# A decoder step on one core: the first stage with half-size first pieces, more warm-up matmuls, small vectors on the GpSimd queue and a pinned order

## Chip, cores and metric

One core of a Trainium2 chip runs the whole step. The metric is device time in microseconds of one execution; the median of several runs is compared. TensorE does the matrix products and transposes, VectorE (DVE), ScalarE (ACT) and GpSimd (POOL) the rest; SyncE (SP), ACT and POOL issue the DMAs.

## What is computed

One layer of a hybrid decoder for 256 prompt tokens and 8 x 8 sample tokens (320 columns in all). The input is normalised, one combined projection feeds two branches (mLSTM and gated linear attention), both are merged by gates, and a gated ConvFFN follows:

```python
h = _rmsnorm(x, norm_mix_w)
proj = h @ _f32(w_in)
mq, mk, mv, mo, mi, mf, gq, gk, gv, gr, gal, gate_a, gate_b = jnp.split(proj, split_at, axis=-1)
...
merged = (jax.nn.sigmoid(gate_a) * (y_m @ _f32(w_branch_a))
          + jax.nn.sigmoid(gate_b) * (y_g @ _f32(w_branch_b)))
x = x + merged @ _f32(w_out)
```

Only the first stage is touched in the source: the load and transposition of x, the token scale `rsqrt(mean(x*x) + EPS)`, and the first two products gq and gk with 256 columns of `w_in` each.

## The kernel before, in words

Every product is done in three passes: a weight block `raw` (128 x 4 x 256, 512 KB) is split by ACT into a rounded part `wh` (line 69) and by DVE into the rest `wl` (line 70); x is kept likewise as `hH[k]` and `hL[k]`, one tile of 128 x 320 for each of 16 row blocks k. TensorE adds `wh*hH`, `wh*hL` and `wl*hH` (lines 74, 75, 76). `raw` has 4 buffers, `wh` and `wl` 3 each, and PSUM has 4 `big` banks (products) and 4 `mx` banks (all else).

The start: 8 warm-up matmuls of ones (line 110), then x is loaded in four column pieces (`x_load`, lines 144 and 145, SP queue), each piece transposed by TensorE in 4 tiles k (`x_chunk`, line 153: two matmuls for the prompt, one for the sample tokens, each recorded as two), from which ACT writes `hH[k]` (154), DVE `hL[k]` (155), and both a plain copy `xT` (158, 160). Weight pieces `first(C_GQ, c)` and `first(C_GK, c)` alternate with the x pieces on SP. A piece c gives 48 products: 4 k x 2 halves x 3 passes for gq, and the same for gk; the stage has 192 products and 16 transposed tiles.

`token_scale` (called for c == 3, lines 163 to 176): ACT squares x with a running sum (168), DVE scales (169), POOL takes the power (170), DVE spreads the result over `lh` (174), TensorE transposes it (175), DVE copies it to `rstd_bc` (176). gq and gk are evacuated with `rstd_bc` (129). Then ten small vectors come in on the SP queue (204 to 213) and are transposed into `vecT` and `cwT` (215 to 217). Behind the stage a gate block `graw` is loaded on the ACT queue and split with POOL's memsets (319, 320) and ACT's small casts (322).

Later, at some 90 to 115 us, the rows `we` (391, 392) are written to DRAM by POOL (403, 404), read back as `bc` (647), and used by DVE in `qi` (658); the same DVE queue frees the PSUM banks of TensorE's level matmuls (568) with predicated copies (571).

What sets the order: the program is recorded in the order of the code, and a scheduler with its own timeline then orders each engine's queue; every engine runs its queue in that order. Eight DMA semaphores for hardware queues go round, so that a ninth issue waits until the transfer eight before it has landed.

Of the kernel before, what the change touches and what calls it, by code (L numbers as in the profile page):

```python
# [24 lines left out]
N = T + NS  # L25
# [7 lines left out]
RAW = 4  # L33
NWARM = 8
# [9 lines left out]
def step_kernel(ctx: ExitStack, tc: tile.TileContext, a: dict):  # L44
# [9 lines left out]
    def mx(name="mx"):  # L54
        return ps.tile([P, 512], F32, tag="mx", name=name)
# [4 lines left out]
    w_in = a["w_in"][0]  # L60

# [40 lines left out]
    nc.vector.memset(onec, 1.0)  # L102
    mhalf = cp.tile([P, 3], F32, name="mhalf")
# [3 lines left out]
    nc.scalar.activation(warm, onec, AF.Copy)  # L107
# [24 lines left out]
    with tc.tile_pool(name="st", bufs=1) as st:  # L132
        vrow = st.tile([P, 3, P], F32, name="vrow")
        nmr = st.tile([16, P], F32, name="nmr")
        nc.scalar.dma_start(nmr, a["norm_mix_w"].rearrange("o (k p) -> (o k) p", p=P))
        nmw = st.tile([P, 16], F32, name="nmw")
        pv = mx("mx1")
        nc.tensor.transpose(pv[:, :16], nmr, ident[0:16, 0:16])
        nc.vector.tensor_copy(nmw, pv[:, :16])
        xn = st.tile([P, 3, DM], F32, name="xn")  # L140

        def x_load(c):
            cs = slice(c * 512, (c + 1) * 512)
            nc.sync.dma_start(xn[:, 0:2, cs], a["x_prompt"][0].rearrange("(b p) c -> p b c", p=P)[:, :, cs])
            nc.sync.dma_start(xn[0:64, 2, cs], a["x_sample"].rearrange("b t c -> (b t) c")[:, cs])

        def x_chunk(c):
            xT = st.tile([P, 4, N], F32, name=f"xT{c}")
            for kk in range(4):
                k = c * 4 + kk  # L150
                pt = mx("mx2")
                for j, (t0, tn) in enumerate(TOK):
                    nc.tensor.transpose(pt[:, t0:t0 + tn], xn[:tn, j, k * P:(k + 1) * P], ident[:tn, :tn])
                nc.scalar.activation(hH[k], pt[:, :N], AF.Copy, scale=nmw[:, k:k + 1])
                nc.vector.scalar_tensor_tensor(hL[k], pt[:, :N], nmw[:, k:k + 1], hH[k].bitcast(F32),
                                               op0=ALU.mult, op1=ALU.subtract)
                if kk % 2:
                    nc.scalar.copy(xT[:, kk], pt[:, :N])
                else:
                    nc.vector.tensor_copy(xT[:, kk], pt[:, :N])  # L160
            nc.gpsimd.dma_start(xT_d[c], xT)

        def token_scale():
# [3 lines left out]
            for j, (t0, tn) in enumerate(TOK):  # L167
                nc.scalar.activation(junk[:tn], xn[:tn, j], AF.Square, accum_out=rs[:tn, j:j + 1])
# [12 lines left out]
        def first(c0, c):  # L181
            return weights(w_in[4 * c * P:4 * (c + 1) * P, c0:c0 + 256], 4, 2)

        x_load(0)
        wq = first(C_GQ, 0)
        x_load(1)
        wkk = first(C_GK, 0)
        x_chunk(0)
        for c in range(4):
            if c < 2:  # L190
                x_load(c + 2)
            if c < 3:
                x_chunk(c + 1)
            if c == 3:
                token_scale()
            part_product(gq_ps, w_in, C_GQ, 4 * c, NK, hH, hL, wq)
            part_product(gk_ps, w_in, C_GK, 4 * c, NK, hH, hL, wkk)
            if c < 3:
                wq, wkk = first(C_GQ, c + 1), first(C_GK, c + 1)
# [4 lines left out]
        nc.sync.dma_start(ibias[0:4], a["mlstm_i_bias"].rearrange("o h -> h o"))  # L204
        nc.sync.dma_start(ibias[32:36], a["mlstm_f_bias"].rearrange("o h -> h o"))
        nc.sync.dma_start(vrow[0:16, 0], a["norm_ffn_w"].rearrange("o (k p) -> (o k) p", p=P))
# [766 lines left out]
```

## Time and profile before

| what | us |
|---|---|
| median of 3 runs | 1939.19 |
| lowest, highest | 1938.01, 1939.68 |
| the profiled execution, its own time | 1938.72 |
| its span, first to last instruction | 1936.1 |
| TensorE busy in it | 1920.9 |

Times in the rows are us from the start of the span. A merged timeline row gives start, busy time, engine, line, operation, tiles and a count; in brackets is the engine's idle time before it and what ended it. Ends of matmuls are modelled, so the pace of TensorE is read from the distance of two starts.

### The profile page before, as it was taken

The numbers are of one execution on the slowest core, as the hardware profiler recorded it, in microseconds if no ns is written. First come the engines' busy times: TensorE is split into PE (matmuls) and PEld (weight loads), VectorE is DVE, ScalarE is ACT, GpSimd is POOL, SyncE is SP. The second block draws the span as 40 slices with busy tenths as digits, with TensorE's granted clock in tenths as the row PEclk, the third lists the DMA queues.
The fourth block names the chain that finished last, engine by engine and source line by source line (L and its number), as shares of the span: only waits on it lengthen the run. The fifth ranks groups of instructions, "written<-read, shape, count | busy, mean of one in ns | idle before, by whom it ended". The sixth has DMA issues, their size and how long they took to land.

```text
span 1936.1 us, 32558 instructions
## 1 busy us (share of the span) xinstructions
PE 1920.9 (99%) x13190; PEld 1893.8 (98%) x13190; DVE 1074.4 (55%) x1598; ACT 782.6 (40%) x1045; POOL 328.0 (17%) x618
## 2 busy tenths in 40 slices
PE   9999999999999999999999999999999999999997
PEld 8999999999999999999999999999999999999997
DVE  5767686867544444445555545544554554555455
ACT  5444443555433333333344334433432443343335
POOL 4223231414000000003121101201110120111014
PEclk9999999999999999999999999999999999999998
DMA  7746665756655555546444444444544444444442
GB/s 237 197 134 186 190 210 171 219 166 208 173 146 150 151 153 151 146 150 207 152 150 146 149 152 152 144 152 152 152 147 148 152 150 149 148 153 152 147 149 95
DMA packets 300223, 311.62 MB, mean 161 GB/s; under 512 B 15264, under 2 KB 292026, under 8 KB 300073
## 3 DMA queue, kind: packets, MB, share of 16 engines
q1 hardware_dynamic: 287849, 283.53, 48.5%
q0 software_dynamic: 7328, 24.50, 3.7%
q8 instruction: 103, 1.69, 0.4%
q10 hardware_dynamic: 4896, 1.52, 0.3%
q14 instruction: 47, 0.39, 0.1%
HBM read 287.03 MB, written 22.48 MB: 160 GB/s over the span
## 4 chain that ended last, share of the span: by engine, by line


## 5 line engine op out<-in xcount | busy, mean ns | idle before, releaser
L70 DVE TENSOR_TENSOR wl<-raw,wh 128x1024 fp32r<-128x1024 f32 x504 | 629.1, 1248 | 627.1 <-ACT wh L69 626.6
L69 ACT ACTIVATE wh<-raw 128x1024 fp32r<-128x1024 f32 x504 | 534.7, 1061 | 866.4 <-PE big L75 742.9
L75 PE MATMUL big<-hL,wh 128*128 128x320 f32 x2832 | 880.4, 311 | 0.0
L74 PE MATMUL big<-hH,wh 128*128 128x320 f32 x2832 | 879.3, 311 | 0.2 <-ACT wh L69 0.2
L76 PE MATMUL big<-hH,wl 128*128 128x320 f32 x2832 | 879.2, 311 | 0.0
L75 PEld LDWEIGHTS big<-hL,wh 128*128 128x128 f32 x2832 | 532.9, 188 | 2.1 <-issue 1.2
L74 PEld LDWEIGHTS big<-hH,wh 128*128 128x128 f32 x2832 | 533.1, 188 | 1.7 <-issue 0.9
L76 PEld LDWEIGHTS big<-hH,wl 128*128 128x128 f32 x2832 | 532.8, 188 | 1.2 <-issue 0.4
L75 PE MATMUL big<-aL,wh 128*128 128x320 f32 x704 | 217.9, 310 | 0.0
L76 PE MATMUL big<-aH,wl 128*128 128x320 f32 x704 | 217.6, 309 | 0.0
L74 PE MATMUL big<-aH,wh 128*128 128x320 f32 x704 | 215.8, 309 | 0.0
L76 PEld LDWEIGHTS big<-aH,wl 128*128 128x128 f32 x704 | 132.4, 188 | 0.0
L75 PEld LDWEIGHTS big<-aL,wh 128*128 128x128 f32 x704 | 132.4, 188 | 0.0
L74 PEld LDWEIGHTS big<-aH,wh 128*128 128x128 f32 x704 | 131.8, 188 | 0.0
L868 POOL COPY conv<-u 128x2 f32<-128x2 f32 x44 | 8.3, 188 | 527.4 <-DVE u L865 527.4
L75 PE MATMUL big<-mL,wh 128*128 128x320 f32 x256 | 78.8, 309 | 0.0
L74 PE MATMUL big<-mH,wh 128*128 128x320 f32 x256 | 78.7, 309 | 0.0
L76 PE MATMUL big<-mH,wl 128*128 128x320 f32 x256 | 78.7, 309 | 0.0
L799 POOL TENSOR_TENSOR g<-g 128x320 f32<-128x320 f32 x16 | 14.6, 913 | 378.1 <-DVE g L795 378.0
L906 DVE TENSOR_TENSOR x<-big,x 128x320 f32<-128x320 f32 x96 | 46.7, 488 | 46.5 <-PE big L76 46.5
L880 POOL TENSOR_TENSOR g<-g,uc 128x256 f32<-128x256 f32 x44 | 32.7, 743 | 211.7 <-DVE g L879 211.5
L75 PE MATMUL big<-yL,wh 128*128 128x320 f32 x192 | 59.2, 308 | 0.0
(356 smaller groups left out, 1798.6 us busy)
## 6 DMA issues: line engine op xcount, KB each, us to landing
raw<-in_w_in SPq DMA_DIRECT2D x176, 512.0 KB, 3.8
raw<-in_ffn_w_up SPq DMA_DIRECT2D x88, 512.0 KB, 3.7
raw<-in_ffn_w_gate SPq DMA_DIRECT2D x88, 512.0 KB, 3.6
raw<-in_ffn_w_down SPq DMA_DIRECT2D x88, 512.0 KB, 3.5
raw<-in_w_out SPq DMA_DIRECT2D x32, 512.0 KB, 3.5
C<-in_state_mlstm_C SPq DMA_DIRECT2D x32, 256.0 KB, 6.2
o_C_s<-C POOLq DMA_DIRECT2D x32, 256.0 KB, 4.7
raw<-in_w_branch_a SPq DMA_DIRECT2D x16, 512.0 KB, 3.5
```

The lines of the kernel that those rows point to most:

```text
L69: nc.scalar.activation(hi, raw, AF.Copy)
L70: nc.vector.tensor_tensor(lo, raw, hi.bitcast(F32), op=ALU.subtract)
L74: nc.tensor.matmul(out, wh, xh, start=first, stop=False)
L75: nc.tensor.matmul(out, wh, xl, start=False, stop=False)
L76: nc.tensor.matmul(out, wl, xh, start=False, stop=last)
L799: nc.gpsimd.tensor_tensor(sg[m], sg[m], acc[m], op=ALU.add)
L868: nc.gpsimd.tensor_copy(conv1[:, 0:2, c], u[:, T:T + 2])
L880: nc.gpsimd.tensor_tensor(g[:, 0:T], g[:, 0:T], gel[m][:, 0:T], op=ALU.mult)
L906: nc.vector.tensor_tensor(x2[k], pt[:, :N], x2[k], op=ALU.add)
```

## The change

Weights and x of the first four row blocks come in halves of two row blocks (256 KB each), the sample rows are laid out as `xs` (two groups of 64 partitions) and loaded by ACT and SP, the later pieces stay at 512 KB. Products of the stage run pass by pass over a half or whole block instead of three passes for each k, and three more warm-up matmuls stand after the first two transposed tiles. `pin` (`tc.keep_in_program_order`) holds transposes, `hH`, `hL`, splits, products, copies and squares in the order of the code among each other; the matmuls of `token_scale` are not pinned. The squares for the sample tokens run over 128 partitions and two groups are added by a matmul with `id2`. The ten small vectors are issued on the GpSimd queue.

```diff
-NWARM = 8
+NWARM = 9
+    pin = tc.keep_in_program_order
+    id2 = cp.tile([P, 64], F32, name="id2")
+    nc.gpsimd.tensor_tensor(id2, ident[:, 0:64], ident[:, 64:128], op=ALU.add)
...
+        def x_load(k0, nk):
+            cs = slice(k0 * P, (k0 + nk) * P)
+            nc.sync.dma_start(xn[:, :, cs], a["x_prompt"][0].rearrange("(b p) c -> p b c", p=P)[:, :, cs])
+        def xs_load(eng, *pairs):
...
+        def x_tiles(k0, nk):
+            pts = []
+            for k in range(k0, k0 + nk):
                 pt = mx("mx2")
...
+                for j in range(2):
+                    pin(nc.tensor.transpose(pt[:, j * P:(j + 1) * P], xn[:, j, k * P:(k + 1) * P], ident))
+                pin(nc.tensor.transpose(pt[:, T:N], xs[r, k // 4 * 2 + k % 2], ident[r, r]))
+                pin(nc.scalar.activation(hH[k], pt[:, :N], AF.Copy, scale=nmw[:, k:k + 1]))
+                pin(nc.vector.scalar_tensor_tensor(hL[k], pt[:, :N], nmw[:, k:k + 1], hH[k].bitcast(F32),
+                                                   op0=ALU.mult, op1=ALU.subtract))
...
         def token_scale():
...
-            for j, (t0, tn) in enumerate(TOK):
-                nc.scalar.activation(junk[:tn], xn[:tn, j], AF.Square, accum_out=rs[:tn, j:j + 1])
+            for j in range(2):
+                pin(nc.scalar.activation(junk, xn[:, j], AF.Square, accum_out=rs[:, j:j + 1]))
+            pin(nc.scalar.activation(junk[:, 0:DM // 2], xs.rearrange("p k c -> p (k c)"), AF.Square,
+                                     accum_out=rs[:, 2:3]))
+            pr = mx("mx3")
+            nc.tensor.matmul(pr[0:64, 0:1], id2, rs[:, 2:3], start=True, stop=True)
+            nc.vector.tensor_copy(rs[0:64, 2:3], pr[0:64, 0:1])
...
+        def rows_split(blk, i, n):
+            c, c0, out, raw, hi, lo = blk
+            pin(nc.scalar.activation(hi[:, i:i + n], raw[:, i:i + n], AF.Copy))
+            pin(nc.vector.tensor_tensor(lo[:, i:i + n], raw[:, i:i + n], hi[:, i:i + n].bitcast(F32), op=ALU.subtract))
+        def rows_product(blk, i, n):
+            c, c0, out, raw, hi, lo = blk
+            for ps_, (w, x) in enumerate(((hi, hH), (hi, hL), (lo, hH))):
+                for m in range(2):
+                    for kk in range(i, i + n):
...
+        xs_load(nc.scalar, 0)
+        nc.scalar.dma_start(nmr, a["norm_mix_w"].rearrange("o (k p) -> (o k) p", p=P))
+        b0, b1 = blocks(0)
+        x_load(0, 2)
+        rows_in(b0, 0, 2)
+        rows_in(b1, 0, 2)
+        x_load(2, 2)
+        xs_load(nc.scalar, 1)
+        rows_in(b0, 2, 2)
+        rows_in(b1, 2, 2)
+        x_load(4, 4)
...
+        pts = x_tiles(0, 2)
+        for _ in range(3):
+            pin(nc.tensor.matmul(pw[:, 0:P], ones, ones, start=True, stop=True))
+        rows_split(b0, 0, 2)
+        rows_split(b1, 0, 2)
+        rows_product(b0, 0, 2)
+        x_keep(pts)
+        pts = x_tiles(2, 2)
+        rows_product(b1, 0, 2)
...
+        for c in range(1, 4):
+            b0, b1 = n0, n1
+            rows_split(b0, 0, 4)
+            pts = x_tiles(4 * c + 2, 2)
+            rows_split(b1, 0, 4)
...
+            rows_product(b0, 0, 4)
+            x_keep(pts)
+            if c < 3:
+                pts = x_tiles(4 * c + 4, 2)
+                rows_product(b1, 0, 4)
+                x_keep(pts)
+            else:
+                token_scale()
+                rows_product(b1, 0, 4)
...
-        nc.sync.dma_start(vrow[0:16, 0], a["norm_ffn_w"].rearrange("o (k p) -> (o k) p", p=P))
+        nc.gpsimd.dma_start(vrow[0:16, 0], a["norm_ffn_w"].rearrange("o (k p) -> (o k) p", p=P))
```

The scheduler turns this into the following queues; a number ahead of a row is its place.

TensorE at the end of the first stage, before: the transposes of `lh` (line 175) stand amid the products, 46 of the stage's 192 still behind them.

```order
194 L76 MATMUL big<-hH_112,wl 128x320
195 L74 MATMUL big<-hH_113,wh 128x320 [waits Activation_49]
196 L75 MATMUL big<-hL_129,wh 128x320 [waits DVE_49]
197 L175 MATMUL mx_479<-ident,lh_480 128x128 [waits DVE_49,PE_49]
198 L175 MATMUL mx_479<-ident,lh_483 128x128
199 L175 MATMUL mx_479<-ident,lh_486 128x64
200 L76 MATMUL big<-hH_113,wl 128x320
```

The same place of the changed kernel (line 187 adds the two groups of sample sums, 195 transposes `lh`, 304 to 306 transpose the small vectors, 227 is the product):

```order
217 L227 MATMUL big<-hH_117,wl 128x320
218 L227 MATMUL big<-hH_118,wl 128x320
219 L187 MATMUL mx_519<-rs,id_78 64x1 [waits PE_49,Activation_49,Pool_49]
220 L195 MATMUL mx_524<-ident,lh_525 128x128 [waits DVE_49,PE_49]
221 L304 MATMUL mx_575<-ident,vrow 128x52 [waits DMASW4_49,DMASW5_49,DMASW3_49,DMASW6_49,DMASW2_49,PE_49]
222 L305 MATMUL mx_575<-ident,vrow 128x88 [waits DMASW7_49]
223 L306 MATMUL mx_575<-ident,vrow 128x88 [waits DMASW1_49,DMASW0_49]
224 L195 MATMUL mx_524<-ident,lh_528 128x128 [waits DVE_49]
225 L195 MATMUL mx_524<-ident,lh_531 128x64 [waits DVE_49]
226 L227 MATMUL big<-hH_115,wh 128x320
227 L227 MATMUL big<-hH_116,wh 128x320
```

The six rows now stand between the last 48 products: 24 (gq, piece 3) ahead of them, 24 (gk, piece 3) behind them.

ScalarE, before: the three squares (line 168) are spread among the casts and `hH` of pieces 2 and 3.

```order
21 L168 ACTIVATE junk,rs<-xn 128x2048
22 L154 ACTIVATE hH_110<-mx_299,nmw 128x320
23 L154 ACTIVATE hH_111<-mx_306,nmw 128x320
24 L69 ACTIVATE wh<-raw 128x1024
25 L168 ACTIVATE junk,rs<-xn 128x2048
26 L154 ACTIVATE hH_112<-mx_313,nmw 128x320
27 L158 COPY xT_291<-mx_299 128x320
28 L69 ACTIVATE wh<-raw 128x1024
29 L312 DMA graw<-in_w_in 128x16x8
30 L168 ACTIVATE junk,rs<-xn 64x2048
```

ScalarE of the changed kernel: `hH_117` and `hH_118` are those of the last two tiles, k = 14 and 15; 218 is the weight cast, 411 the cast of the gate block, 183 and 184 the squares.

```order
36 L163 ACTIVATE hH_117<-mx_472,nmw 128x320
37 L163 ACTIVATE hH_118<-mx_478,nmw 128x320
38 L218 ACTIVATE wh<-raw 128x1024
39 L411 ACTIVATE wh<-graw 128x8x4 x2
40 L411 ACTIVATE wh<-graw 128x8x16
41 L172 COPY xT_149<-mx_478 128x320
42 L183 ACTIVATE junk,rs<-xn 128x2048
43 L411 ACTIVATE wh<-graw 128x8x4 x2
44 L411 ACTIVATE wh<-graw 128x8x16
45 L183 ACTIVATE junk,rs<-xn 128x2048
46 L184 ACTIVATE junk,rs<-xs 128x1024
```

All three squares now stand behind the last `hH` and the last cast of the stage, with the gate block's casts between them.

VectorE behind the read of `bc` (line 658 before, 747 now), before:

```order
114 L571 COPY_PREDICATED AT<-lvl_622,mx_1007 128x64
115 L658 TENSOR_TENSOR qi<-q,bc 128x128
116 L660 COPY dec<-bc 128x8
117 L678 TENSOR_TENSOR qn<-qi,n0T 128x64 x2
118 L663 TENSOR_TENSOR nT<-n0T,dec 128x2x8
119 L70 TENSOR_TENSOR wl<-raw,wh 128x1024
120 L501 COPY qz<-qi 128x2x4x8
121 L556 TENSOR_TENSOR lv_d<-gb_755 128x40x4
122 L557 TENSOR_TENSOR lv_d<-gb_755 128x40x4
123 L129 SCALAR_TENSOR_TENSOR k<-big,rstd_bc 128x320
124 L571 COPY_PREDICATED AT<-lvl_628,mx_1019 128x2x32
```

And now:

```order
116 L660 COPY_PREDICATED AT<-lvl_643,mx_1028 128x64
117 L747 TENSOR_TENSOR qi<-q,bc 128x128
118 L749 COPY dec<-bc 128x8
119 L767 TENSOR_TENSOR qn<-qi,n0T 128x64 x2
120 L645 TENSOR_TENSOR lv_d<-gb_776 128x40x4
121 L646 TENSOR_TENSOR lv_d<-gb_776 128x40x4
122 L752 TENSOR_TENSOR nT<-n0T,dec 128x2x8
123 L590 COPY qz<-qi 128x2x4x8
124 L660 COPY_PREDICATED AT<-lvl_649,mx_1040 128x2x32
125 L71 TENSOR_TENSOR wl<-raw,wh 128x1024
```

The weight split and the evacuation of k that stood between `qi` and the copy for the second level (`lvl_628`, now `lvl_649`) have moved behind that copy.

## Rows read from the trace of the kernel before

**Rows 1.** The page: span, busy time by engine (us, share, instructions)
```profile
span 1936.1 us, 32558 instructions
...
PE 1920.9 (99%) x13190; PEld 1893.8 (98%) x13190; DVE 1074.4 (55%) x1598; ACT 782.6 (40%) x1045; POOL 328.0 (17%) x618
```
**Rows 2.** Waits of TensorE: in total us, times, longest
```profile
PE mx L568 <- DVE AT L571: 1.6, 1, 1.6
```
**Rows 3.** Timeline of TensorE, first 20 us
```profile
1.12 3.78 PE L110 MATMUL mx<-ones 128*128 128x128 f32 x16 [1.12 <-DVE onec L102]
5.05 3.34 PE L153 MATMUL mx<-ident,xn 128*128 128x128 f32 x12
8.55 0.64 PE L74 MATMUL big<-hH,wh 128*128 128x320 f32 x1 [0.15 <-ACT wh L69]
...
10.64 0.63 PE L76 MATMUL big<-hH,wl 128*128 128x320 f32 x1
...
13.47 0.38 PE L75 MATMUL big<-hL,wh 128*128 128x320 f32 x1
...
16.79 1.15 PE L153 MATMUL mx<-ident,xn 128*128 128x128 f32 x6
17.87 0.42 PE L76 MATMUL big<-hH,wl 128*128 128x320 f32 x1
18.12 0.31 PE L74 MATMUL big<-hH,wh 128*128 128x320 f32 x1
...
19.14 0.31 PE L75 MATMUL big<-hL,wh 128*128 128x320 f32 x1
```
**Rows 4.** Timeline of ScalarE, first 13 us
```profile
6.50 0.53 ACT L154 ACTIVATE hH<-mx,nmw 128x320 fp32r<-128x320 f32 x1 [3.70 <-PE mx L153]
7.44 1.06 ACT L69 ACTIVATE wh<-raw 128x1024 fp32r<-128x1024 f32 x1 [0.41 <-DMA raw<-in_w_in]
```
**Rows 5.** Timeline of ScalarE, 27 to 41 us
```profile
27.34 1.90 ACT L168 ACTIVATE junk<-xn 64x2048 f32<-64x2048 f32 x1
29.14 0.19 ACT L168 ACTIVATION_READ_ACCUMULATOR junk<-xn 64x1 f32 x1
...
36.57 0.42 ACT L158 COPY xT<-mx 128x320 f32<-128x320 f32 x1
...
40.28 0.55 ACT L322 ACTIVATE wh<-graw 128x32 fp32r<-128x32 f32 x3 [1.90 <-POOL wh L319]
```
**Rows 6.** Timeline of VectorE, 28 to 32 us, the end of the token scale
```profile
29.45 0.17 DVE L169 TENSOR_SCALAR rs<-rs 128x3 f32<-128x3 f32 x1 [0.74 <-ACT junk L168]
30.63 0.68 DVE L174 TENSOR_SCALAR lh<-ones,rs 128x128 f32<-128x128 f32 x3 [1.01 <-POOL rs L170]
```
**Rows 7.** Timeline of TensorE, 38 to 48 us, without products
```profile
39.51 0.97 PE L175 MATMUL mx<-ident,lh 128*128 128x128 f32 x6
47.35 0.26 PE L215 MATMUL mx<-ident,vrow 52*128 52x52 f32 x1
```
**Rows 8.** Timeline of TensorE, 105 to 113 us, around its one long wait
```profile
105.78 0.31 PE L75 MATMUL big<-hL,wh 128*128 128x320 f32 x1
107.73 0.43 PE L568 MATMUL mx<-lv_z 128*128 128x64 f32 x2 [1.63 <-DVE AT L571]
107.97 0.39 PE L76 MATMUL big<-hH,wl 128*128 128x320 f32 x1
```
**Rows 9.** Windows: length, busy us (count) of PE, PEld, DVE, ACT, POOL, granted clock, DMA
```profile
109.20:112.60 3.40, 3.40 (x14) 3.40 (x15) 3.07 (x7) 1.03 (x2) 2.44 (x3) 0.50 0.45 120
```
**Rows 10.** Timeline of VectorE, 100 to 113 us
```profile
104.65 0.29 DVE L658 TENSOR_TENSOR qi<-q,bc 128x128 f32<-128x128 f32 x1 [3.22 <-DMA bc<-rows]
...
105.35 1.21 DVE L70 TENSOR_TENSOR wl<-raw,wh 128x1024 fp32r<-128x1024 f32 x1
...
107.05 0.48 DVE L129 SCALAR_TENSOR_TENSOR k<-big,rstd_bc 128x320 f32<-128x320 f32 x1
107.45 0.36 DVE L571 COPY_PREDICATED AT<-lvl,mx 128x64 f32<-128x64 uint8 x2
```

More of the change, by code (lines that the diff above doesn't have):

```diff
@@ L147, in x_chunk @@
[L147 to L150, printed above, removed]
-                pt = mx("mx2")
-                for j, (t0, tn) in enumerate(TOK):
[L153 to L158, printed above, removed]
-                else:
-                    nc.vector.tensor_copy(xT[:, kk], pt[:, :N])
-            nc.gpsimd.dma_start(xT_d[c], xT)
+        xn = st.tile([P, 2, DM], F32, name="xn")
@@ new lines, in step_kernel @@
+        xs = st.tile([P, NK // 2, P], F32, name="xs")
+        xT = [st.tile([P, 4, N], F32, name=f"xT{c}") for c in range(4)]
+        def x_load(k0, nk):
+            cs = slice(k0 * P, (k0 + nk) * P)
+            nc.sync.dma_start(xn[:, :, cs], a["x_prompt"][0].rearrange("(b p) c -> p b c", p=P)[:, :, cs])
+        def xs_load(eng, *pairs):
+            src = a["x_sample"].rearrange("b t c -> (b t) c")
+            for i in pairs:
+                r = 64 * (i % 2)
+                eng.dma_start(xs[r:r + 64, i // 2 * 2:i // 2 * 2 + 2].rearrange("p k c -> p (k c)"),
+                              src[:, 2 * i * P:2 * (i + 1) * P])
@@ L163, in token_scale, with x_keep @@
+        def x_keep(pts):
+            for k, pt in pts:
+                if k % 2:
+                    pin(nc.scalar.copy(xT[k // 4][:, k % 4], pt[:, :N]))
+                else:
+                    pin(nc.vector.tensor_copy(xT[k // 4][:, k % 4], pt[:, :N]))
+                if k % 4 == 3:
+                    nc.gpsimd.dma_start(xT_d[k // 4], xT[k // 4])
         def token_scale():
@@ L179, in step_kernel, with blocks @@
         gk_ps = [big(), big()]
[L181 to L191, printed above, removed]
-            if c < 3:
-                x_chunk(c + 1)
-            if c == 3:
+        def blocks(c):
+            t = []
+            for c0, out in ((C_GQ, gq_ps), (C_GK, gk_ps)):
+                raw = ring.tile([P, 4, 256], F32, tag="raw", name="raw", bufs=RAW)
+                hi = ring.tile([P, 4, 256], F32R, tag="wh", name="wh", bufs=3)
+                lo = ring.tile([P, 4, 256], F32R, tag="wl", name="wl", bufs=3)
+                t.append((c, c0, out, raw, hi, lo))
+            return t
@@ new lines, in rows_product @@
+        def rows_product(blk, i, n):
+            c, c0, out, raw, hi, lo = blk
+            for ps_, (w, x) in enumerate(((hi, hH), (hi, hL), (lo, hH))):
+                for m in range(2):
+                    for kk in range(i, i + n):
+                        k = 4 * c + kk
+                        pin(nc.tensor.matmul(out[m][:, :N], w[:, kk, m * P:(m + 1) * P], x[k],
+                                             start=(k == 0 and ps_ == 0), stop=(k == NK - 1 and ps_ == 2)))
+        xs_load(nc.scalar, 0)
@@ new lines, in step_kernel @@
+        nc.scalar.dma_start(nmr, a["norm_mix_w"].rearrange("o (k p) -> (o k) p", p=P))
+        pin(nc.scalar.activation(warm, onec, AF.Copy))
+        b0, b1 = blocks(0)
[7 more added lines that the diff above has]
+        x_load(4, 4)
+        xs_load(nc.scalar, 2, 3)
+        n0, n1 = blocks(1)
+        rows_in(n0, 0, 4)
+        rows_in(n1, 0, 4)
+        x_load(8, 4)
@@ new lines, in step_kernel @@
+        xs_load(nc.sync, 4, 5)
+        pv = mx("mx1")
+        pin(nc.tensor.transpose(pv[:, :16], nmr, ident[0:16, 0:16]))
+        pin(nc.vector.tensor_copy(nmw, pv[:, :16]))
+        pts = x_tiles(0, 2)
[7 more added lines that the diff above has]
+        rows_product(b1, 0, 2)
+        rows_split(b0, 2, 2)
```

51 lines of the change are left out of this document (27 added, 24 removed).

## The prediction

> **What bounds the kernel now.** The page comes first: TensorE is busy for 1920.9 of 1936.1 us [rows 1], no other engine comes near it, so only what makes TensorE wait or run slowly counts. The waits of TensorE come second: one wait of 1.6 us, for a predicated copy of DVE, and nothing else of weight [rows 2]. The timeline of the first 20 us comes third. A busy TensorE hides there that it is slow: two products start 0.27 us apart up to 13.5 us (8.55 to 13.47, with transposes between) and 0.146 us apart later (18.12 to 19.14, seven steps) [rows 3]. So TensorE ran at 1.2 GHz until 13.6 us and at 2.4 GHz after it. It rose 2.95 us after the last interruption (10.64) and 5.0 us after the first product (8.55). The windows come fourth: the granted clock is 0.50 from 109.2 to 112.6 us [rows 9], right behind the one long wait, which ended at 107.73 [rows 8]. The same loss thus has two faces, a wait and then some us at half speed. The whole recoverable time is a few us; the change works at the start and, through the order, at two places behind it.
>
> **1. The start.** *Warm-up.* Eight matmuls are 16 records in 3.78 us [rows 3], 0.236 each, so 0.472 for one; nine end at 1.12 + 4.25 = 5.37 instead of 4.90. *Transposes.* A tile k costs 3.34 / 4 = 0.835 at the low clock [rows 3], and a pair 17.87 - 16.79 = 1.08 at the high one, 0.54 each. With 0.15 for the transposition of the norm weights, as now between 4.90 and 5.05, two tiles run from 5.5 to 7.2, the three added matmuls (1.42) to 8.65. *Pieces.* They are not on the path: the full first x piece is there at 5.05 now, the full first weight piece at 7.44 [rows 3, 4], and ACT cannot take a weight piece before it has done the second `hH`, whose tile ends at 7.2: 7.25 + 0.53 = 7.8. The half cast lies between 0.53 (320 elements) and 1.06 (1024) [rows 4]; by the line through both it is 0.67, so 8.5. The first product starts at about 8.65 against 8.55. The pieces may land earlier by 1 us or more, and it buys nothing. If a half piece came later than 8.5, each us late would cost a half us at the low clock.
>
> *Clock.* From 7.2 us on TensorE has no gap, warm-up and products alike. At the distance of the row (2.95) the clock rises at 10.2 instead of 13.6. Count the work done by 13.6 in full-speed time. Before: 15 products and 5 tiles, 15 x 0.146 + 5 x 0.54 = 4.9 us. After: 2 tiles (1.1), then 1.5 us at half speed (0.8), then 3.4: 5.3 us. Gain 0.4. If the clock rises at 13.6 as before, it is 1.1 + 4.95 / 2 = 3.6, a loss of 1.3. I take -0.3, as small waits for the second `hH` of a pair return some; bounds -0.4 and +1.3. The remaining stage has the same 192 products and 16 tiles, and TensorE has no waits of note in it now; ACT and DVE keep room, as their squares leave it.
>
> **2. The token scale, the largest term.** Let X be the end of the transposes of tiles 14 and 15. The order puts 24 products behind X, 24 x 0.146 = 3.5 us, and then TensorE's queue holds the matmul on the squares' sums, with the last 24 products behind it. The squares stand on ACT behind everything that depends on X. ACT from X: second `hH` 0.6; cast 1.06 (1.65); gate casts 0.55 (2.2); copy 0.42 (2.6); square 1.90 + 0.19, 1.99 with the overlap (4.6); gate casts 0.55 (5.15; POOL's memset for them starts at X + 3.5, in time); square (7.15); the square of 1024 elements, about a cast of that size and 0.19 (8.4) [rows 4, 5]. Then the added matmul and DVE copy, some 0.4 (an estimate, two short steps like the 0.17 of the scaling row [rows 6]), and the chain as measured: accumulator read out at 29.33, `lh` at 30.92 for the first and 31.31 for the last, 2.0 us [rows 5, 6], and the last transposition 0.3: X + 11.1. TensorE stood from X + 3.5, 7.6 us. In it lie 1.6 us of work that is paid elsewhere now, the `lh` transposes (0.97) and the three for the small vectors (47.35 on, 0.6) [rows 7]. **Added: 6.0 us.** Bounds: 5.0, if the added matmul and copy cost nothing and the squares overlap more; 7.0, if the gate casts wait for POOL, whose queue also holds a DMA issue there. Before, the same squares ended at 29.33 and the transposes ran at 39.51: ten us of cover, all gone. The small vectors have nothing to do with it; they are issued at the start of POOL's queue, ten short issues, and nobody needs POOL then except `ident`, which is ahead of them.
>
> **3. The clock behind that wait.** A wait of 1.63 us was enough for 3.4 us at half clock [rows 8, 9]. After 7.6 us with a few small matmuls the clock will be low when the products resume, and by the two distances at the start it rises 2.95 to 5.0 us later. Half of that is lost: 1.5 to 2.5, I take **+2.0**.
>
> **4. The wait at 106 us.** TensorE reached the level matmul at 106.1 and got it at 107.73, when DVE had made the copy for the second level at 107.45 to 107.67 [rows 8, 10]. DVE had stood at `qi` until `bc` landed (104.65) and then ran a split (1.21) and an evacuation (0.48) ahead of that copy. By the order both are now behind it: -1.7. The fourth gate product comes 3 products earlier and its last step no longer stands behind a split: the chain to `bc` is 0.4 + 1.2 = 1.6 us earlier against TensorE, whose 178 products from the first gate product to the gate transposes are the same count. So the copy is made at about 104.3 on the old clock. TensorE has 57 instead of 64 products ahead of the matmul and arrives 1.0 earlier, at 105.1. Slack 0.8: the wait goes, and with it the half-clock stretch, 1.63 + 3.4 / 2 = **-3.3**. The bound is 0, if `bc`, a DMA round trip, is 1 us later. What is late next is the copy for the third level, now right behind the split, with 12 products (1.8 us) of cover.
>
> **Sum.** The profiled execution took 1938.72. -0.3 + 6.0 + 2.0 - 3.3 = +4.4, so 1943.1; the median of the runs lies 0.47 above that execution: **1943.6**.
>
> **The rivals.** *The wait at 106 us stays.* For it: it hangs on a DMA landing and 0.8 us of slack; DVE has two more evacuations and one more split ahead of `qi`. Against it: these fit into the 3.22 us that DVE stood idle there. Then 1943.6 + 3.3 = 1946.9.
>
> *An early clock.* The warm-up is longer, and with luck the clock rises at its end, 5.4 us. Then tiles take 0.54, the added matmuls 0.7, ACT has the first cast at 7.9, and by 13.6 TensorE has done 1.1 + 5.7 = 6.8 us of work, 1.9 more than before: 1943.6 - 1.6 = 1942.0. Against it: 3.78 us of warm-up did not raise it in this execution [rows 3], and 4.25 is little more. The Trainium skill, TensorE: Matmul & The Clock Gate, section "What's actually happening", says that the chip's look at activity runs freely and does not begin with the kernel, so that the rise falls differently from run to run; by that rule some executions would take this course, and one profile cannot show it.
>
> *TensorE does not stand at the token scale.* This one ends on the other side. It is so if the queue lets the 24 ready products pass the waiting matmul, or if those ahead of it take longer than ACT's 11 us; the point is 3.5 us of cover against 11.1. Terms 2 and 3 vanish: 1939.2 - 0.3 - 3.3 = 1935.6, and 1934 with the early clock. Against it: at 106.1 the queue stood still though the product next behind the wait ran without one [rows 8]. The Trainium skill, Perfetto Trace Analysis, section "Tensor Engine Instruction (MATMUL, LD_WEIGHTS)", grants TensorE a limited reorder that pulls weight loads ahead of matmuls in flight; if that reached ready products too, this rival's time would be the result. The trace shows nothing of the kind.
>
> **How the numbers follow.** Forecast 0.52, by itself 1942.0 to 1945.5; the wait at 106 stays 0.25; early clock 0.12; no wait at the token scale 0.08; new waits in the reordered part up to 440 us 0.03. The range leaves out the third rival below and the upper end of the first above: 1938.5 to 1948.0. A measurement here tells about 0.2% from no change, 3.9 us, that is 1935.3 and 1943.1. Slower: 0.35 of the forecast, 0.25, 0.01 and 0.03, 0.64. Faster: half of the no-wait rival, 0.04, and 0.01 for what I don't see, 0.05. The rest, 0.31, is within.
>
> **What would show it.** Right: line 195 or 187 in the waits of TensorE, together 5 us or more, released by ACT's squares and DVE's `lh`; a window at 0.50 right behind it, near 50 us; no wait near 106 us; the first product near 8.6 us. Wrong: the matmul of line 187 starts right behind the 24 products, or the first product starts before 7.5 us, so that the pieces were on the path after all.

## The result and the profile after

The changed kernel takes 1946.2 us (median of 6 runs, 1945.8 to 1946.8) against 1939.6 us for the kernel before on the same chip: ratio 1.0037, 95% interval 1.0025 to 1.0048. It is slower, by some 7 us. Run again it gave 1.0039 (1.0026 to 1.0052). One run of a later version (the norm weights first) took 3802.8 us, for a reason that nothing here shows, and its ratio goes by the six others. The profiled execution took 1945.81 us with a span of 1943.4 us, 7.3 us more than the span before.

Its busy times on the page, to be held against [rows 1]:

```profile
PE 1923.7 (99%) x13200; PEld 1894.8 (97%) x13200; DVE 1076.7 (55%) x1601; ACT 781.5 (40%) x1047; POOL 336.0 (17%) x629
```

TensorE is busy for 2.8 us more. The four added warm-up matmuls (4.21 and 1.65 us now, rows below, 3.78 before [rows 3]) and the matmul of the row sum (0.25) make 2.3 of it, so the busy time tells little of the 7 us. The waits of TensorE in the changed kernel (engine, tile, line, what it waited for: sum, times, longest). The one wait of before [rows 2] is nearly gone (line 657 now, 0.2 us), and two others stand above it:

```profile
PE mx L187 <- issue: 3.8, 1, 3.8
PE mx L195 <- DVE lh L194: 1.9, 1, 1.9
PE mx L113 <- DVE onec L103: 1.1, 1, 1.1
PE mx L250 <- DMA nmr<-in_norm_mix_w: 0.5, 1, 0.5
PE mx L657 <- DVE AT L660: 0.2, 1, 0.2
```

Lines 187 and 195 are the row sum and the spreading transposes of the token scale. The timeline of ACT from the last pair of tiles on shows what holds them (start, busy time, engine, line, operation; in brackets the idle time before):

```profile
39.38 1.10 ACT L163 ACTIVATE hH<-mx,nmw 128x320 fp32r<-128x320 f32 x2 [1.61 <-PE mx L162]
40.38 1.05 ACT L218 ACTIVATE wh<-raw 128x1024 fp32r<-128x1024 f32 x1
41.33 0.53 ACT L411 ACTIVATE wh<-graw 128x32 fp32r<-128x32 f32 x3
41.76 0.41 ACT L172 COPY xT<-mx 128x320 f32<-128x320 f32 x1
42.06 1.92 ACT L183 ACTIVATE junk<-xn 128x2048 f32<-128x2048 f32 x1
...
44.41 1.90 ACT L183 ACTIVATE junk<-xn 128x2048 f32<-128x2048 f32 x1
...
46.44 1.06 ACT L184 ACTIVATE junk<-xs 128x1024 f32<-128x1024 f32 x1
47.40 0.19 ACT L184 ACTIVATION_READ_ACCUMULATOR junk<-xs 128x1 f32 x1
```

Before, the last square ended at 29.33 [rows 5], ten us ahead of the transposes that need it at 39.51 [rows 7]. Now it ends at 47.59, and TensorE's queue stands behind it. TensorE over the same stretch:

```profile
47.69 0.25 PE L187 MATMUL mx<-rs,id 128*64 128x1 f32 x2 [3.81 <-issue]
49.84 0.77 PE L195 MATMUL mx<-ident,lh 128*128 128x128 f32 x2 [1.90 <-DVE lh L194]
50.53 0.35 PE L304 MATMUL mx<-ident,vrow 52*128 52x52 f32 x1
...
51.16 1.32 PE L195 MATMUL mx<-ident,lh 128*128 128x128 f32 x4
...
52.40 2.50 PE L227 MATMUL big<-hH,wh 128*128 128x320 f32 x8
54.70 1.53 PE L227 MATMUL big<-hL,wh 128*128 128x320 f32 x8
56.06 1.33 PE L227 MATMUL big<-hH,wl 128*128 128x320 f32 x8
57.24 0.31 PE L75 MATMUL big<-hH,wh 128*128 128x320 f32 x1
```

The first group of eight products takes 2.30 us from start to start, the third 1.18: the clock changes under them. The windows (stretch and its length, TensorE busy with its count, granted clock, DMA share, GB/s) say where:

```profile
43.70:47.70 4.00, 0.18 (x3) 1.00 0.98 314
47.70:52.50 4.80, 2.90 (x12) 0.56 1.05 326
52.50:55.10 2.60, 2.60 (x10) 0.50 1.10 350
55.10:60.00 4.90, 4.90 (x35) 1.00 0.77 237
109.20:112.60 3.40, 3.35 (x25) 1.00 0.31 76
```

The half clock at 109.2 us of before [rows 9] is gone; one at 48.3 to 55.1 has come. At the place of the old wait DVE still stands for `bc`, but the copy that TensorE needs is made right behind, and TensorE stands 0.24 us instead of 1.63 [rows 8, 10]. DVE, then TensorE:

```profile
107.71 0.29 DVE L747 TENSOR_TENSOR qi<-q,bc 128x128 f32<-128x128 f32 x1 [2.68 <-DMA bc<-rows]
...
108.97 0.22 DVE L660 COPY_PREDICATED AT<-lvl,mx 128x64 f32<-128x64 uint8 x1
```

```profile
109.25 0.43 PE L657 MATMUL mx<-lv_z 128*128 128x64 f32 x2 [0.24 <-DVE AT L660]
```

The start of the stage completes the picture, TensorE in its first 10 us:

```profile
1.12 4.21 PE L113 MATMUL mx<-ones 128*128 128x128 f32 x18 [1.12 <-DVE onec L103]
5.83 0.26 PE L250 MATMUL mx<-ident,nmr 16*128 16x16 f32 x1 [0.50 <-DMA nmr<-in_norm_mix_w]
...
7.85 1.65 PE L254 MATMUL mx<-ones 128*128 128x128 f32 x6
9.15 1.41 PE L227 MATMUL big<-hH,wh 128*128 128x320 f32 x4
```

The first product comes at 9.15 instead of 8.55 [rows 3]. Later in the stage TensorE's weight loads (PEld) wait three times for the second `hH` of a pair, at 21.1, 30.9 and 40.5 us, 0.7 us in all; the kernel before has no such wait. The last of them:

```profile
40.53 0.73 PEld L227 LDWEIGHTS big<-hH,wh 128*128 128x128 f32 x5 [0.24 <-ACT hH L163]
```

Where the time went, by the starts of the same products in the two traces: the 168 products ahead of the token scale are done at 43.71, the same number of before at 43.74 including 0.97 for the transposes of line 175, so +0.94; the stand at the token scale, 43.71 to 52.40, is 8.69, less the 0.97 and the 0.44 that `vecT`'s transposes cost before, +7.28; the last 24 products take 4.84 instead of 3.52, +1.32. The first product behind the stage's 192 is then 9.54 us late (57.24 against 47.70), the one behind 3000 only 7.0 (579.23 against 572.23): -2.54 between, where the wait at 106 us lies. The last product of the program is again 7.0 us late.

### The profile page after: what moved, and what is told of

The parts are those of the page before. It is cut to its first block, busy times and chain, and to the rows that moved or that the text cites. A ratio compares the mean times of both kernels' runs of the same rounds, so it can differ in the third digit from the quotient of the medians.

```text
span 1943.4 us, 32582 instructions
## 1 busy us (share of the span) xinstructions
PE 1923.7 (99%) x13200; PEld 1894.8 (97%) x13200; DVE 1076.7 (55%) x1601; ACT 781.5 (40%) x1047; POOL 336.0 (17%) x629
## 3 DMA queue, kind: packets, MB, share of 16 engines
q1 hardware_dynamic: 287824, 283.15, 48.3%
## 4 chain that ended last, share of the span: by engine, by line
PE 98%; issue 0%; DMA 0%; ACT 0%; POOL 0%; DVE 0%; POOLq 0%; ACTq 0%
PE big L76 30%; PE big L77 30%; PE big L75 30%; PE big L227 1%; PE mxi L596 1%; PE mx L566 1%; PE mx L657 1%; PE mx L576 0%; PE mx L814 0%; PE mx L569 0%; PE mx L568 0%; PE mx L161 0%; PE mx L527 0%; DMA bc<-rows 0%; PE mx L609 0%
## 5 line engine op out<-in xcount | busy, mean ns | idle before, releaser
L71 DVE TENSOR_TENSOR wl<-raw,wh 128x1024 fp32r<-128x1024 f32 x496 | 619.6, 1249 | 618.0 <-ACT wh L70 617.7
L70 ACT ACTIVATE wh<-raw 128x1024 fp32r<-128x1024 f32 x496 | 525.8, 1060 | 873.1 <-PE big L76 738.5
L76 PE MATMUL big<-hL,wh 128*128 128x320 f32 x2768 | 859.7, 311 | 0.0
L75 PE MATMUL big<-hH,wh 128*128 128x320 f32 x2768 | 858.2, 310 | 0.0
L77 PE MATMUL big<-hH,wl 128*128 128x320 f32 x2768 | 857.5, 310 | 0.0
L76 PEld LDWEIGHTS big<-hL,wh 128*128 128x128 f32 x2768 | 519.8, 188 | 2.6 <-issue 2.1
L77 PEld LDWEIGHTS big<-hH,wl 128*128 128x128 f32 x2768 | 519.7, 188 | 0.9 <-issue 0.4
L75 PEld LDWEIGHTS big<-hH,wh 128*128 128x128 f32 x2768 | 519.7, 188 | 0.4
L77 PE MATMUL big<-yH,wl 128*128 128x320 f32 x192 | 59.2, 308 | 0.0
```

What stands on the lines that cost most here:

```text
L70: nc.scalar.activation(hi, raw, AF.Copy)
L71: nc.vector.tensor_tensor(lo, raw, hi.bitcast(F32), op=ALU.subtract)
L75: nc.tensor.matmul(out, wh, xh, start=first, stop=False)
L76: nc.tensor.matmul(out, wh, xl, start=False, stop=False)
L77: nc.tensor.matmul(out, wl, xh, start=False, stop=last)
```

## Experiments

Each was timed against the kernel before on its own chip. A ratio near 1.0037 means: as the changed kernel. Edits are to the changed kernel unless another is named.

**The squares early.** The three squares go between the tiles of c == 1 and c == 2, and the token scale is cut into row sum and spreading with 16 products between them.

```diff
+            if c == 2:
+                square(0)
...
+            square(2 if c == 1 else 1)
...
-            token_scale()
-            rows_product(b1, 0, 4)
+            token_sum()
+            rows_product(b1, 0, 4, (0, 1))
+            token_spread()
+            rows_product(b1, 0, 4, (2,))
```

> Theory (the two late squares on ACT and the row sum behind them hold TensorE, and its clock falls behind that): with the squares earlier on ACT and the row sum cut in three between products, the waits of 3.81 us and 1.90 us ahead of the row sum and the spreading transposes go (under 0.5 us each), the clock stays at 1.00 from 48 to 55 us, and the last 24 products take 3.5 us instead of 4.84. From 1946.2 that takes 7.3 + 1.3 = 8.6 us: about 1937.6, if nothing later gives it back; if the wait of 1.6 us at 106 us returns with the half clock behind it (3.3 us in the kernel before), about 1940.9. Rival (the half-size pieces, the eight transfers or the vectors on the GpSimd queue cost the time, and the wait only shows it): at least 1944.

Measured: ratio 1.0002 (0.9994 to 1.0011), 1938.6 us against 1937.9. The waits at the token scale are gone; the wait of the kernel before is back, with its half clock. As ratios the two figures of the expectation are 0.9990 and 1.0007, and the second, with that wait, lies within the interval. First its waits, then the wait in the timeline:

```profile
PE mx L670 <- DVE AT L673: 1.8, 1, 1.8
PE mx L113 <- DVE onec L103: 1.1, 1, 1.1
PE mx L258 <- DMA nmr<-in_norm_mix_w: 0.7, 1, 0.7
```

```profile
105.80 1.01 PE L670 MATMUL mx<-lv_z 128*128 128x64 f32 x4 [1.76 <-DVE AT L673]
```

So the token scale, with its squares late and no products between its steps, is the whole loss within the interval; what the squares and the cut are worth each by itself isn't shown. From the last product ahead of the row sum to the first behind the stage TensorE takes 5.98 us instead of 13.68, 7.7 of the 8.6 us that the stand and the clock behind it cost. Why the wait at 106 us is back, DVE's queue shows:

```profile
103.13 0.29 DVE L760 TENSOR_TENSOR qi<-q,bc 128x128 f32<-128x128 f32 x1 [2.34 <-DMA bc<-rows]
...
103.92 1.22 DVE L71 TENSOR_TENSOR wl<-raw,wh 128x1024 fp32r<-128x1024 f32 x1
...
105.53 0.68 DVE L673 COPY_PREDICATED AT<-lvl,mx 128x64 f32<-128x64 uint8 x3
```

The weight split stands between `qi` and the copy again. From `qi` to the copy it is 2.40 us here, 2.80 before [rows 10] and 1.26 in the changed kernel. That TensorE was 9.5 us late behind the stage shows no part in it: it reached the waiting matmul 0.91 us after `qi` began here, 1.45 before and 1.30 in the changed kernel.

**All products first.** The last 24 products ahead of the token scale.

```diff
-                token_scale()
                 rows_product(b1, 0, 4)
+                token_scale()
...
-            nc.tensor.matmul(pr[0:64, 0:1], id2, rs[:, 2:3], start=True, stop=True)
+            pin(nc.tensor.matmul(pr[0:64, 0:1], id2, rs[:, 2:3], start=True, stop=True))
```

> Theory: the same row sum with all 24 remaining products ahead of it. ACT's chain ends where it did (row sum at 47.7 us), the products fill 3.5 us of the wait of 3.81 us, the clock falls no earlier than 47 us and the half-clock stretch of some 6.8 us lands on the products of the next weights instead. Saved: 3.5 us; given back: about 1 us, since the next products need a PSUM buffer that is read out only after the scale is spread. About 1943.7 (1942 to 1945). Rival (the wait is not what costs the time): 1946.2 within 0.7.

Measured: 1.0034 (1.0022 to 1.0046), 1944.6 us. The waits fell to 1.1 and 1.9 us, and 1.2 us at the next product, for the PSUM bank, came as forecast:

```profile
55.70 0.61 PE L75 MATMUL big<-hH,wh 128*128 128x320 f32 x1 [1.20 <-DVE gq L132]
```

But the gain of 2.5 us did not come whole. The start was 1.2 us later than in the changed kernel (44.78 against 43.56 at the last product that both have ahead of the row sum, a later rise of the clock). At this line the kernel was 1.5 us ahead (55.70 against 57.24), like for like 2.8; 48 products on it was 1.0 us behind (65.30 against 64.28), like for like 0.2 ahead. These 48 took 9.60 us instead of 7.04: the half clock lasted 10.2 us here, 50.95 to 61.19, instead of 6.8, and lay on full work. Most of what the cover gained was paid back at half clock behind the wait. That stretch also lasted 10.2 us, and the clock also rose late (13.2 us), when the changed kernel was run again (below). Against that execution this one was 3.4 us ahead at this line (55.70 against 59.08) and still 1.6 at the last product (1928.74 against 1930.33).

**Filler in the wait.** 13 and 6 matmuls on ones in front of the row sum and of the spreading.

```diff
+            pf = mx("mx3")
+            for _ in range(13):
+                pin(nc.tensor.matmul(pf[:, 0:P], ones, ones, start=True, stop=True))
-            nc.tensor.matmul(pr[0:64, 0:1], id2, rs[:, 2:3], start=True, stop=True)
+            pin(nc.tensor.matmul(pr[0:64, 0:1], id2, rs[:, 2:3], start=True, stop=True))
+            for _ in range(6):
+                pin(nc.tensor.matmul(pf[:, 0:P], ones, ones, start=True, stop=True))
...
-                nc.tensor.matmul(pr[:, t0:t0 + tn], lh[:tn], ident[:tn, :tn], start=True, stop=True)
+                pin(nc.tensor.matmul(pr[:, t0:t0 + tn], lh[:tn], ident[:tn, :tn], start=True, stop=True))
```

> Theory: 13 and 6 matmuls on ones stand in the two waits (0.275 us each at full clock: 3.6 and 1.65 us of 3.81 and 1.90), so TensorE has no idle stretch there and the clock stays at 1.00. The waits themselves stay, the work behind them runs at full clock: the 24 products in 3.5 us instead of 4.84 (-1.3), the four spreading matmul instructions and three transposes in about half of their 2.5 us (-1.1). About 1943.8 (1943 to 1944.6). Rival (the clock falls for another reason than the idle stretch): clock 0.50 stays, 1946.2 or up to 0.5 later.

Measured: 1.0031 (1.0020 to 1.0043), 1943.85 us. At the place itself it is right: the clock stayed up and the first product behind the stage came at 54.74 instead of 57.24, 2.5 us earlier, of which the start had brought 0.2 (43.35 against 43.56 at the last product ahead of the row sum); 2.4 were forecast. In the profiled execution it was lost again at 68 us; these are its windows:

```profile
51.10:54.70 3.60, 3.60 (x25) 1.00 1.09 360
54.70:68.20 13.50, 13.50 (x86) 1.00 0.74 222
68.20:75.10 6.90, 6.90 (x23) 0.51 0.27 78
```

The clock fell at 68.2 us, with TensorE shown busy for the 13.5 us ahead, just behind the first matmuls with only 16 rows of weights (line 440, six records from 65.54). In the changed kernel the same matmuls run at 68.04 and nothing falls. Some 100 products on (the one behind 300) the kernel was 0.55 us later than the changed one (77.00 against 76.45). So the price of the clock behind the wait is shown (2.3 us with the token scale's own matmuls). Whether filler can keep it isn't: the profiled execution took 1945.4 us, the longest of six (the others 1942.8 to 1944.1), and no trace tells whether the clock fell there in the others.

**The vectors back on SP.**

```diff
-        nc.gpsimd.dma_start(vrow[0:16, 0], a["norm_ffn_w"].rearrange("o (k p) -> (o k) p", p=P))
+        nc.sync.dma_start(vrow[0:16, 0], a["norm_ffn_w"].rearrange("o (k p) -> (o k) p", p=P))
...
```

> Theory: the ten small vectors' queue is on no path. 1946.2 within 1, the waits at the row sum as they are. Rival (their transfers on the GpSimd queue hold the pow of the row sum, the vector transposes or the stores of xT): 1944 or less. Other rival (on the SP queue they hold the weights again): 1948 or more.

Measured: 1.0038 (1.0026 to 1.0051). Within the interval the queue of the vectors costs and brings nothing.

**Whole pieces again.**

```diff
-        x_load(0, 2)
-        rows_in(b0, 0, 2)
-        rows_in(b1, 0, 2)
-        x_load(2, 2)
+        x_load(0, 4)
+        rows_in(b0, 0, 4)
+        rows_in(b1, 0, 4)
...
-        rows_in(b0, 2, 2)
-        rows_in(b1, 2, 2)
```

> The first rows of x and of the two weight blocks loaded in whole pieces again (512 KB of weights each), all else as in the changed kernel. Theory: the half-size pieces are on no path, since the first product waits for ACT (hH, hH, then the first weight cast at 8.4 us) and not for the weights (landed at 5.5 and 6.5 us); a whole block can land up to 2 us later and still be in time. First product at 9.2 us within 0.5, ratio to the kernel before 1.0037 within 0.0008, as the changed kernel. Rival (the pieces bring the data in time and hide another loss): first product at 10 us or later and at least 1 us more at the end, ratio 1.0042 or above.

Measured: 1.0044 (1.0031 to 1.0056), first product at 10.20 us. My expectation missed, and the rival's figures came out, by a way that neither had named. TensorE at its start:

```profile
6.88 0.26 PE L247 MATMUL mx<-ident,nmr 16*128 16x16 f32 x1 [1.55 <-DMA nmr<-in_norm_mix_w]
```

The norm weights (8 KB), second on ACT's queue, come 0.8 to 1.05 us later than with halves (6.88 against 5.83 to 6.07 in eight executions). They are issued at 1.42 us in both and land at 6.75 instead of 5.70, with larger transfers under way beside them; which of these holds them isn't shown. The halves thus do bring about 1 us at the first product, not through the weights that they carry but through a small transfer that lands earlier beside them; the timed difference to 1.0037 alone would not show it.

**Eight warm-up matmuls, none added.**

```diff
-NWARM = 9
+NWARM = 8
...
-        for _ in range(3):
-            pin(nc.tensor.matmul(pw[:, 0:P], ones, ones, start=True, stop=True))
```

> Eight warm-up matmuls and none of the three added ones. Theory: these stand in time in which TensorE waits anyway (between 7.9 and 9.15 us), so without them the first product comes no earlier (9.15 us within 0.3); if they brought the clock up, it now rises near 13.6 us as in the kernel before instead of 10.7, which leaves some 3 us more of the first products at half clock: +1.5 us, ratio 1.0045. Rival A (the clock's first rise has nothing to do with them): rise anywhere between 5.5 and 13.5 us, as in the four runs that already have them, and ratio 1.0037 within 0.0008. Rival B (they delay the products): first product 0.5 us earlier, ratio 1.0033 or below.

Measured: 1.0046 (1.0033 to 1.0058), first product at 9.06 us, clock up at 12.7 us. The added matmuls stand in idle time, as said, and delay nothing. Whether they bring the clock up earlier stays open: the ratio can't be told from 1.0037, and 12.7 us lies among the moments seen with them (below).

**The norm weights first on ACT's queue.**

```diff
-        xs_load(nc.scalar, 0)
         nc.scalar.dma_start(nmr, a["norm_mix_w"].rearrange("o (k p) -> (o k) p", p=P))
+        xs_load(nc.scalar, 0)
```

> The norm weights ahead of the sample rows on ACT's queue. Theory: the wait of 0.5 us for them ahead of the first transpose goes; the sample rows come one place later (about 5.7 us instead of 4.4), so the first tile's last transpose waits for them instead and at most 0.3 us is won: first product at 8.85 to 9.2 us, end within 0.5 us of the changed kernel. Rival (the late norm weights are the whole reason why the first product came 0.5 us later than forecast): first product at 8.65 us.

Measured: 1.0031 (1.0020 to 1.0042). It brought more than either figure: no wait for the norm weights any more, 0.2 us for the sample rows, first product at 7.58 us.

```profile
4.78 0.23 PE L250 MATMUL mx<-ident,nmr 16*128 16x16 f32 x1
...
7.58 0.85 PE L227 MATMUL big<-hH,wh 128*128 128x320 f32 x4 [0.27 <-ACT wh L218]
```

Not all of the 1.57 us is the transfer: the clock was up from 4.2 us in this execution, so the warm-up ended early too. With the usual warm-up (below, with the other edits) their transposition starts at 5.26, 0.57 us earlier than at 5.83, and that is the transfer's part.

**The changed kernel once more.**

> The changed kernel as it is, once more. Theory: the first rise of TensorE's clock is not set by the program, so the same instructions see it elsewhere than at 10.74 us by a microsecond or more, and the start (the last product ahead of the row sum) moves by half the difference; the waits of 3.8 and 1.9 us at the row sum are the same within 0.1 us; ratio 1.0037 within 0.0008. Rival (the rise follows the warm-up and the products): 10.7 us within 0.2.

Measured: 1.0039. The waits at the token scale are 3.8 and 1.9 us again; the clock rose at 13.2 us. The same products in the timeline of this run, four from start to start in 1.06 us ahead of that moment and in 0.68 behind it:

```profile
11.60 1.27 PE L227 MATMUL big<-hH,wl 128*128 128x320 f32 x4
12.66 0.63 PE L161 MATMUL mx<-ident,xn 128*128 128x128 f32 x2
...
14.00 0.84 PE L227 MATMUL big<-hH,wh 128*128 128x320 f32 x4
14.68 0.60 PE L227 MATMUL big<-hL,wh 128*128 128x320 f32 x3
```

It is the identical program, so the program does not fix the moment. The product ahead of the row sum started at 44.78 instead of 43.56, 1.2 us later, half of the 2.5 us by which the clock rose later. At the old wait, now at 111 us, this execution stood 1.0 us instead of 0.2: it reached the matmul 0.56 us after `qi` began, not 1.30.

**`qi` behind the level copies**, on top of the early squares.

```diff
+        def pin0(h, op):
+            if h == 0:
+                pin(op)
...
-                    nc.vector.copy_predicated(
+                    pin0(h, nc.vector.copy_predicated(
...
-            nc.vector.tensor_tensor(qi, q[:, :, T:], bc[:, N:N + 64].unsqueeze(1).broadcast_to([P, 2, 64]), op=ALU.mult)
+            pin0(h, nc.vector.tensor_tensor(qi, q[:, :, T:], bc[:, N:N + 64].unsqueeze(1).broadcast_to([P, 2, 64]), op=ALU.mult))
...
```

> The version with the squares early, and on VectorE the two readers of the broadcast rows of the first mLSTM head (qi and dec) pinned behind the level copies of the first GLA head, so that VectorE no longer stands 2.3 us for that transfer in front of them. Theory: the wait of 1.76 us at 104 us goes, and the half clock of 3.4 us behind it (1.7 us): 3.4 us less than with the squares early alone, which had a ratio of 1.0002; so 0.9984 (0.9978 to 0.999), faster than both kernels. Rival (the wait is the level chain's own length on VectorE, ScalarE and GpSimd): the wait stays over 1 us with another cause, ratio 1.0002 within 0.0006.

Measured: 0.9989 (0.9980 to 0.9998), 1935.9 us against 1938.6. The wait fell to 0.64 us, for GpSimd, and no half clock follows it; the products from 192 to 3000 take 521.2 us instead of 524.1 with the squares early alone. The profiled execution was the longest of 11 (1939.2; the others 1934.7 to 1938.6): its clock rose at 13.7 us.

**That, and the norm weights first.**

```diff
-        xs_load(nc.scalar, 0)
         nc.scalar.dma_start(nmr, a["norm_mix_w"].rearrange("o (k p) -> (o k) p", p=P))
+        xs_load(nc.scalar, 0)
```

> Squares early, qi behind the level copies, and the norm weights ahead of the sample rows on ACT's queue. Theory: the last one starts the first product 0.8 to 1.6 us earlier than 9.38 us and keeps it to the end, as with the norm weights first alone (ratio 1.0031 against 1.0037): 0.9982 against 0.9989 without it. Rival (the earlier start is lost to a wait before 45 us): first product earlier, the 192nd product where it was for the same rise of the clock, 0.9989.

Measured: 0.9980 (0.9971 to 0.9988); the norm weights are transposed at 5.26 us, right behind the warm-up, and the first product comes at 8.15 us, with the clock up from 6.3 us. It points the way expected; against the run before the intervals overlap.

**`qi` behind the level copies in the kernel before**, with the same edit and nothing of the change.

> The kernel before, with nothing of the change, but VectorE's two readers of the broadcast rows (qi and dec of the first mLSTM head) pinned behind the level copies of the first GLA head. Theory: the wait of 1.63 us at 106 us and the half clock of 3.4 us behind it are worth 3.3 us by themselves and hang on the place of qi alone: ratio 0.9983 (0.9978 to 0.9990). Rival (the next step of that chain is just as late, or the half clock comes somewhere else): ratio 1.0 within 0.0006, with another wait over 1 us or a stretch at 0.50 near 110 us.

Measured: 0.9980 (0.9971 to 0.9989), 1936.0 us against 1939.8. The time is the theory's, and the one profile is the rival's. It took 1939.78 us, the longest of its 11 runs (the others 1934.5 to 1937.0), and has a wait of 1.82 us for `lv_z` and a half clock behind it. It was also 1.6 us late at the first product behind the stage (49.33 against 47.70), as its clock fell at 9.7 us and rose again only at 16.5. GpSimd there:

```profile
102.27 0.64 POOL L651 DMA_DIRECT2D bc<-rows  x1 [3.52 <-DMA rows<-R]
102.93 1.28 POOL L563 TENSOR_TENSOR lv_z<-gk,lv_d 128x128 f32<-128x128 f32 x1
104.18 0.44 POOL L564 TENSOR_TENSOR lv_z<-gq,lv_d 128x128 f32<-128x128 f32 x1
```

GpSimd stands in front of the load of `bc` until the store of the rows has landed, and the level products are queued behind it.

**The load of `bc` behind the level products as well**, again in the kernel before.

```diff
-                nc.gpsimd.tensor_tensor(z4[:, :, 0], k4[:, :, 0], d4[:, :, 0], op=ALU.mult)
+                pin0(h, nc.gpsimd.tensor_tensor(z4[:, :, 0], k4[:, :, 0], d4[:, :, 0], op=ALU.mult))
...
-            nc.gpsimd.dma_start(bc, rows_d[h:h + 1].broadcast_to([P, 776]))
+            pin0(h, nc.gpsimd.dma_start(bc, rows_d[h:h + 1].broadcast_to([P, 776])))
```

> The kernel before with qi and dec pinned behind the level copies, as in the run before, and now on GpSimd the load of the broadcast rows (bc) pinned behind the level products (lv_z) of the first GLA head. Theory: what was left there in the profiled execution of the run before, a wait of 1.82 us for lv_z, came from GpSimd's queue, which stood 3.5 us in front of that load until the store of the rows had landed; with the load behind them nothing at 100 to 112 us waits for a transfer any more: no wait over 0.6 us there, no stretch at 0.50 near 105 us, products 192 to 3000 in about 521.2 us instead of 524.5, ratio 0.9980 or up to 0.0005 less. Rival (the level chain itself is too long for TensorE's cover): a wait over 1 us stays between 100 and 115 us. Second rival (bc is late for the first mLSTM head): a new wait between 120 and 200 us.

Measured: 0.9983 (0.9974 to 0.9992), 1935.4 us. The products from 192 to 3000 take 520.85 us instead of 524.53, and the windows show TensorE without a gap and at full clock:

```profile
100.00:105.00 5.00, 5.00 (x39) 1.00 0.62 164
105.00:110.00 5.00, 5.00 (x39) 1.00 0.56 148
```

Of these 3.7 us a wait of 0.45 us at 448.2 us, which the kernel before has and this one has not (its line 695), is a part further on; the place itself is worth 3.3 us. That the load needed moving rests on the one profile of the run before; the times of the two (0.9980 and 0.9983) do not tell them apart. This kernel and the two ahead of it are faster than both kernels of the case, and can't be told apart; two of the three have nothing of the change.

## Why the prediction was right, and where it was not

1946.2 us against a forecast of 1943.6, within the range, on the side named. On the profiled spans the sum was +4.4 and came out as +7.0 at the last product.

- **The start, -0.3 forecast, +0.94 measured; this is the term that failed.** The step "two tiles run from 5.5 to 7.2" took the norm weights to be there when the warm-up ended. They had been moved to second place on ACT's queue, and TensorE got them 0.5 us after it was free, at 5.83. So the first product came at 9.15, not 8.65. With this and the rise at 10.7 the forecast's own count of the work done by 13.6 us gives 4.75 us instead of 5.3: 0.55. Larger is a part that the sum took at 0.1, "small waits for the second `hH` of a pair": they are three of 0.24, 0.7 us. Together that is nearly all of the 1.2 us between forecast and result. The price of a tile, 0.835, holds: the 12 records of [rows 3] are four tiles, for each transposition is one record in the trace, not the two that the description of the kernel gives it. That the clock rose at 10.7 us in this execution, close to the 10.2 forecast, was luck. With a rise at 13.2, near that of before, the same program stood at 44.78 + 0.15 where before, without line 175, stood at 42.77: +2.2, and my bound for that case was +1.3. In the repetition the first product came at 9.32 and the three waits were the same. "It buys nothing" of the pieces held for the weights and missed what whole pieces do to the small transfers (1.05 us at the first transpose).
- **The token scale, +6.0 forecast, +7.3 measured.** The mechanism is as described: X at 39.9 us, ACT's last accumulator out at 47.6, X + 7.7 (forecast 8.4), the chain behind it to the last transpose at 52.4, X + 12.5 (forecast 11.1). The squares came earlier than my sum by the overlaps. From ACT's last accumulator to the first transpose of `lh` it was 2.25 us, where the sum has 2.0. What I missed stands behind that: the queue puts all of the spreading and the vector transposes in a row there, at half clock, 2.56 us from 49.84 to 52.40, where the sum has 0.3 behind the last `lh`. The early squares gave back 7.7 us of what this term and the next had cost.
- **The clock behind it, +2.0 forecast, +1.32 measured** on the 24 products. With the part that lies on the token scale's own matmuls, counted in the term above, it is 2.3 us, as the filler showed at that place.
- **The wait at 106 us, -3.3 forecast, -2.54 measured.** Wait and half clock went, and for the reason given: with the split and the evacuation behind it, the copy is made 1.26 us after `qi` begins instead of 2.80, 1.54 of the 1.7 in the sum, and with the split back between them the wait returned at 1.76 us (squares early). The other part failed: `bc` was to come 0.6 us earlier against TensorE, but TensorE reached the matmul 1.30 us after `qi` began instead of 1.45. So there was no slack of 0.8 us but a wait of 0.24, and 1.0 in the repetition. Wait (1.39) and half clock (1.7) are 3.1 us, and the 0.45 us at 448 us is gone here too; about 1.0 us was lost elsewhere in the reordered part, in no wait of TensorE, and where isn't shown.

Of the rivals, the wait at 106 us came as a shadow only (0.2 us, and 1.0 in the repeated run, without a half clock). The early clock is real: the version with the vectors on SP had it at 5.6 us and was 1.5 us ahead of the changed kernel before the row sum, where I had 1.6. TensorE stopped at the token scale for 3.8 us with 24 products behind the waiting matmul, in all six profiled executions with that order; the rival in which they pass it fell.

## What to carry to other kernels

A pin fixes what an engine does last as well as first: before pinning a side computation, find its reader in the queue of the engine that bounds the kernel, and count the cover between them. Before, a scheduler's order had ten us there, the pinned one 3.5. When a wait of one or two us sits on an otherwise busy TensorE, look on the other engines for an instruction that reads a round trip through memory long before anyone needs it, and put it behind the work that TensorE wants. Whether the load itself must move too rests here on one profile.

## What the runs showed of the hardware that I had not expected

The moment at which TensorE's clock first rises is not fixed by the program: with the changed kernel's order of start it was 10.7, 13.2, 10.6, 13.4, 10.2, 13.8 and (vectors on SP) 5.6 us, and with the start of before 13.6 and 16.0; one execution of that start rose at 6.3, fell at 9.7 and rose again at 16.5. Each us of it is half a us at the token scale (1.2 for 2.5 in the repeated run), so one profile can't price a change to the start to better than some 2 us. The Trainium skill, TensorE: Matmul & The Clock Gate, section "What's actually happening", says that the look at activity runs freely and does not start with the kernel; the repeated run agrees, 13.2 against 10.7 us for one program. The spread that the section gives with it, plus or minus half a us, is too small for these runs.

The clock can also fall while the trace shows TensorE busy throughout: 68.2 to 75.1 us in the version with filler, behind matmuls with only 16 rows of weights. That they are the cause isn't shown: in the changed kernel they run too and nothing falls, and no run here settles why. And half-clock stretches behind the same wait differ from execution to execution: 6.8 us in the changed kernel, 10.2 us in its repetition.
